# A hybrid decoder layer on one core: side work placed by a time model, the delta rule cut in two, 256-column weight blocks, scratch transfers on ScalarE's queue

## The chip, the core and the metric

The kernel runs on one core of a Trainium2 chip. The core has a matrix engine (TensorE, PE in the profile, with its weight loads as PEld), three engines for element-wise work (VectorE = DVE, ScalarE = ACT, GpSimd = POOL) and a synchronisation engine (SyncE = SP), which here issues DMA transfers. The metric is the device time of one execution in microseconds; lower is better. Before the change it is 1955.09 us, the median of three runs (1952.89 to 1960.22).

## What is computed

One inference step of one layer for two request groups that share all weights: a prompt of 256 tokens and 8 requests with one token each. Everything is float32.

```python
h = rmsnorm(x, norm_mix)
proj = h @ w_in                       # 2048 x 13344: pool, q, k, v, z, a, b, two gates
A = pool_mixer(proj[pool])            # trailing means over 2, 4, 8, 16 tokens, small products
q, k, v = silu(short_conv(proj[qkv])) # causal, width 4; q, k l2-normalised per head (16 heads of 128)
o, S = gated_delta_chunked(q, k, v, g, beta, S0)
#   per chunk: a_mat = strict_lower((k*beta) @ k.T * decay)
#              sol = solve(a_mat + I, [v*beta | k*beta*exp(gc)]); then products with S and q
gdn = rmsnorm(o) * silu(z)
x += (sig(gp)*(A @ w_pool_up) + sig(gg)*(gdn @ w_gdn_up)) @ w_o
x += (silu(f @ w_gate) * (f @ w_up)) @ w_down          # f = rmsnorm(x), inner width 5632
x += (p @ w_ple) * sig(x @ w_ple_gate);   y = rmsnorm(x)
```

It returns the 264 output rows and the new pooling, convolution and delta-rule states.

## The kernel before

**Weight products.** All 264 tokens are the moving columns of every matrix product. The weights come from memory in 592 blocks of 512 KB, two 128-row tiles by 512 columns each. `wload` (L244) issues a block on SP's queue into one of three buffers `wr`. `split` writes the rounded high part `wh` on ACT (L174) and the rest `wl` on DVE (L158), four buffers each. `gemm` then runs 24 products of 128x128x264 per block on PE (L183): each of 8 weight tiles gives high by high, high by low and low by high into an accumulator `acc`. There are about 14,160 of these products. Four accumulators of 512 columns are filled over all blocks of a column stripe, then evacuated.

**Side work.** All the rest (norms, convolution, delta rule, mixer, gates, state stores) is written as Python generators that hand back a step at a time. `tick`, called after each group of six products, moves these generators on by fixed counts of such slots (`yield -3` means three slots later, constants `W1` to `WD`) and by a budget of PE work. The scheduler then sets the order of each engine, except where program order is kept: PE's side products and transposes, SP's side DMAs, and everything on the side engines in the first of four head groups.

**The delta rule** (`gdn`) runs once for each of four groups of four heads, beside the weight products of the q, k, v and z stripes. Its chain of steps: the decay masks `dm`; transposes `kv` and products `pp` on PE; the matrix A (in `dm`). Then the diagonal 32x32 blocks of A are inverted on POOL: four DMAs of 32 KB put them in a scratch tensor `scr`; one DMA of 512 KB, named g<-scr, reads the 128 KB of `scr` four times over into 128 partitions; 31 dependent steps of a multiply and a subtract on POOL (L161, L158); a copy (L777); a DMA to a second scratch (scr<-g); four DMAs back (g<-scr, x4); a 32x32 transpose on DVE (L786). PE's products `px` and `py` then double the blocks to 128, and further products give outputs and states (`pu`, `po`, `pS`, `pk`, `pq`). All DMAs named here are on SP's queue. The last tokens of q, k and v leave by small tiles `tl`, filled by POOL (L626, L627), transposed on PE (`tlp`) and stored.

**After the delta rule** come the mixer, the sample tokens' delta rule (`kqp` and `pd` on PE, its states `S` loaded and stored in 512 KB pieces), the merges, out_proj, the feed-forward part and the embedding part.

Of the kernel before, what the change touches and what calls it, by code (L numbers as in the profile page):

```python
# [15 lines left out]
# slots between dependent steps of the work beside the weight products  # L16
W1, W2, W3 = 6, 3, 8
WA, WB, WC, WD = 5, 5, 6, 2
# [10 lines left out]
KB = 2  # L29
JS = 2  # L30
NL = 5
SIDE = ("DVE", "Activation", "Pool")
# [3 lines left out]
GH = 4  # L36


class Step:
    def __init__(self, ctx, tc, ins, outs):  # L40
# [8 lines left out]
        self.accp = ctx.enter_context(tc.tile_pool(name="accp", bufs=5, space=ps))  # L49
        self.psp = ctx.enter_context(tc.tile_pool(name="psp", bufs=3, space=ps))  # L50
        self.dp = ctx.enter_context(tc.tile_pool(name="dp", bufs=2, space=bass.MemoryType.DRAM))
        self.n = 0
        self.lanes = []
# [3 lines left out]
        self.wait = 0  # L57
        self.rate = 0.5
        self.budget = 0.0
        self.strm = self.stream()  # L60
        self.raws, self.pre = [], []
        self.LA, self.LD, self.LM = 1, 1, 3
        self.pins = SIDE
        self.nsp = 0
# [7 lines left out]
    # Keeps what was traced since n0 in program order on its engine.  # L72
    def pin(self, n0):
        ins = self.nc.cur_bb.bb.instructions
        for k in range(n0, len(ins)):
            e = ins[k].engine
            if str(e).split(".")[-1] in self.pins:
                for j in range(k - 1, -1, -1):
                    if ins[j].engine == e:
                        self.tc.add_manual_dep(ins[k], ins[j].name, mybir.DependencyInfo(  # L80
                            mybir.DependencyClass.NoSync, mybir.DependencyReason.DATA), reason="order")
                        break

    def step(self, gen):
        n0 = self.count()
        c = next(gen, None)
        self.pin(n0)
        if c is None:
            return True, 0
        if c > 0:  # L90
            self.budget -= c
            return False, 0
        return False, int(-c)

    def tick(self):
        self.budget = min(self.budget + self.rate, 2 * self.rate)
        for lane in list(self.lanes):
            lane[1] -= 1
            if lane[1] > 0:
                continue  # L100
            done, lane[1] = self.step(lane[0])
            if done:
                self.lanes.remove(lane)
        if self.post and self.budget > 0:
            cost, fn = self.post.pop(0)
            n0 = self.count()
            fn()
            self.pin(n0)
            self.budget -= cost
        if self.wait > 0:  # L110
            self.wait -= 1
        while self.main and self.budget > 0 and not self.wait:
            done, self.wait = self.step(self.main[0])
            if done:
                self.main.pop(0)

    def lane(self, gen):
        self.lanes.append([gen, 0])

    def drain(self):  # L120
        while self.post or self.lanes or self.main:
            self.budget = 1e9
            if self.post:
                self.post.pop(0)[1]()
# [5 lines left out]
        self.budget, self.wait = 0.0, 0  # L130
# [48 lines left out]
    def dma(self, out, in_):  # L179
        self.tc.keep_in_program_order(self.nc.sync.dma_start(out, in_))  # L180

    def mm(self, out, lhsT, rhs, start=True, stop=True, pin=True):
        ins = self.nc.tensor.matmul(out, lhsT, rhs, start=start, stop=stop)  # L183
        if pin:
            self.tc.keep_in_program_order(ins)

    def tr(self, out, in_):
        k = in_.shape[0]
        self.tc.keep_in_program_order(self.nc.tensor.transpose(out=out, in_=in_, identity=self.ident[:k, :k]))  # L189
# [10 lines left out]
    def stream(self):  # L200
# [3 lines left out]
        def cols(src, r0, K, c0, n=512):  # L204
            for k in range(0, K, KB):
                yield src, r0 + k, min(KB, K - k), c0, n
        wi = lambda c0: cols(w_in, 0, KT, c0)
        for hg in range(4):
            for part in (1, 0, 2, 3):
                yield from wi(1024 + part * D + hg * 512)  # L210
# [27 lines left out]
    def wload(self):  # L238
# [4 lines left out]
        raw = self.wp.tile([P, KB, 512], F32, tag="wr", name=self.nm("wr"), bufs=3)[:, :nk, :n]  # L243
        self.nc.sync.dma_start(raw, src[k0 * P:(k0 + nk) * P, c0:c0 + n].rearrange("(k p) c -> p k c", p=P))  # L244
        self.raws.append((raw, nk, n))

    def wsplit(self):
        n0 = self.count()
        raw, nk, n = self.raws.pop(0)
        hi = self.wp.tile([P, KB, 512], F32R, tag="wh", name=self.nm("wh"))[:, :nk, :n]  # L250
        lo = self.wp.tile([P, KB, 512], F32R, tag="wl", name=self.nm("wl"))[:, :nk, :n]
# [3 lines left out]
        if self.nsp == 1:  # L255
            self.pin(n0)
# [16 lines left out]
    def gemm(self, K, xh, xl, evac):  # L273
        accs = [self.accp.tile([P, 512], F32, tag="acc", name=self.nm("acc"))[:, :NT] for _ in range(4)]
        for k0 in range(0, K, KB):
            nk = min(KB, K - k0)
            wh, wl = self.wblock()
            for m in range(4):
                for kk in range(nk):
                    k = k0 + kk  # L280
                    h = wh[:, kk, m * P:(m + 1) * P]
                    l = wl[:, kk, m * P:(m + 1) * P]
                    self.mm(accs[m], h, xh[:, k], start=(k == 0), stop=False, pin=False)
                    self.mm(accs[m], h, xl[:, k], start=False, stop=False, pin=False)
                    self.mm(accs[m], l, xh[:, k], start=False, stop=(k == K - 1), pin=False)
                if k0 + nk == K:
                    evac(m, accs[m])
                self.tick()

    # ------------------------------------------------------------ constants  # L290
# [50 lines left out]
    def params2(self):  # L341
# [6 lines left out]
        yield -8  # L348
# [51 lines left out]
    # ------------------------------------------------------------ input norm  # L400
# [24 lines left out]
    def input_norm(self, x, xs):  # L425
# [50 lines left out]
        yield -4  # L476
# [9 lines left out]
    # ------------------------------------------------------------ decays  # L486
    def decays(self):
# [9 lines left out]
        yield -5  # L497
# [12 lines left out]
        ab = pool.tile([P, 3, 32], F32, name="ab", bufs=1)  # L510
# [15 lines left out]
        while self.post:  # L526
            yield -1
# [4 lines left out]
        yield -2  # L532
# [17 lines left out]
        yield -2  # L550
# [9 lines left out]
        g3 = pool.tile([P, 3, 32], F32, name="g3", bufs=1)  # L560
# [19 lines left out]
        self.dm = self.B("dm")[:, :H * TP].rearrange("p (h b c) -> p h b c", h=H, b=2)  # L580

        def mask(q):
            rm = self.e4("gm", F32R)[:96, :512].rearrange("p (j t) -> p j t", j=4)
# [919 lines left out]
```

## Time and profile before

| | |
|---|---|
| runs | 1952.89, 1955.09, 1960.22 us |
| span of the profiled execution, first to last instruction | 1954.1 us |
| PE busy | 1883.0 us, 96% of the span |
| weight loads | 1858.6 us, 95% |
| DVE, ACT, POOL busy | 1097.2 us (56%), 875.1 us (45%), 326.7 us (17%) |
| DMA | 344.93 MB, 177 GB/s on average |
| mean granted clock of PE | 0.982 of full speed |

The profiled execution's own time is its span, 1954.1 us, and what lies around it; the span is 1.0 us under the median of the runs. Busy times of different engines overlap and don't add up to the span. PE's clock has two levels here, 2.4 GHz (1.0) and 1.2 GHz (0.5), and a mean between them says for what share of a stretch each was granted.

### The profile page before, as it was taken

The numbers are of one execution on the slowest core, as the hardware profiler recorded it, in microseconds if no ns is written. First come the engines' busy times: TensorE is split into PE (matmuls) and PEld (weight loads), VectorE is DVE, ScalarE is ACT, GpSimd is POOL, SyncE is SP. The second block draws the span as 40 slices with busy tenths as digits, with TensorE's granted clock in tenths as the row PEclk, the third lists the DMA queues.
The fourth block names the chain that finished last, engine by engine and source line by source line (L and its number), as shares of the span: only waits on it lengthen the run. The fifth ranks groups of instructions, "written<-read, shape, count | busy, mean of one in ns | idle before, by whom it ended". The sixth has DMA issues, their size and how long they took to land.

```text
span 1954.1 us, 38176 instructions
## 1 busy us (share of the span) xinstructions
PE 1883.0 (96%) x15700; PEld 1858.6 (95%) x15700; DVE 1097.2 (56%) x1724; ACT 875.1 (45%) x1408; POOL 326.7 (17%) x628
## 2 busy tenths in 40 slices
PE   8998997989989999999999999999999999999997
PEld 7998997989989888999999999999999999999997
DVE  5764655646644876745565555544545544555554
ACT  6573543535534343444444444433444333444444
POOL 1325243251431322200011000000000000000011
PEclk9998998999989999999999999999999999999998
DMA  7555454544646678765655666556666556665553
GB/s 230 178 149 151 137 155 125 152 144 147 165 125 189 208 215 268 209 183 179 227 181 170 180 182 183 178 180 183 181 177 182 183 180 178 182 183 179 178 173 110
DMA packets 219058, 344.93 MB, mean 177 GB/s; under 512 B 26003, under 2 KB 65756, under 8 KB 218740
## 3 DMA queue, kind: packets, MB, share of 16 engines
q1 hardware_dynamic: 218883, 342.50, 58.8%
q8 instruction: 123, 2.02, 0.4%
q14 instruction: 52, 0.42, 0.1%
HBM read 327.28 MB, written 16.03 MB: 176 GB/s over the span
## 4 chain that ended last, share of the span: by engine, by line
PE 79%; DMA 7%; POOL 6%; issue 3%; DVE 2%; ACT 2%; SPq 0%; ACTq 0%; DVEq 0%; POOLq 0%
PE acc L183 74%; POOL g L158 3%; DMA g<-scr 3%; POOL g L161 2%; DMA out_dram<-S 2%; DMA wr<-in_w_in_dram 1%; DMA S<-in_state_ssm_dram 1%; PE pp L183 1%; PE px L183 1%; DVE wl L158 1%; ACT wh L174 1%; PE py L183 0%; SPq L180 0%; PE kv L189 0%; PE po L183 0%
## 5 line engine op out<-in xcount | busy, mean ns | idle before, releaser
L158 DVE TENSOR_TENSOR wl<-wr,wh 128x1024 fp32r<-128x1024 f32 x592 | 727.3, 1229 | 666.2 <-ACT wh L174 665.4
L174 ACT ACTIVATE wh<-wr 128x1024 fp32r<-128x1024 f32 x592 | 625.0, 1056 | 863.0 <-PE acc L183 666.1
L183 PE MATMUL acc<-hh,wh 128*128 128x264 f32 x1664 | 488.2, 294 | 0.4 <-ACT wh L174 0.4
L183 PE MATMUL acc<-hl,wh 128*128 128x264 f32 x1664 | 478.6, 288 | 0.0
L183 PE MATMUL acc<-hh,wl 128*128 128x264 f32 x1664 | 477.4, 288 | 0.0
L183 PE MATMUL acc<-xnh,wh 128*128 128x264 f32 x1408 | 400.4, 284 | 0.0
L183 PE MATMUL acc<-xnl,wh 128*128 128x264 f32 x1408 | 400.2, 284 | 0.0
L183 PE MATMUL acc<-xnh,wl 128*128 128x264 f32 x1408 | 400.1, 284 | 0.0
L183 PEld LDWEIGHTS acc<-hh,wh 128*128 128x128 f32 x1664 | 319.2, 192 | 4.0 <-issue 2.0
L183 PEld LDWEIGHTS acc<-hl,wh 128*128 128x128 f32 x1664 | 319.2, 192 | 1.2 <-issue 0.2
L183 PEld LDWEIGHTS acc<-hh,wl 128*128 128x128 f32 x1664 | 317.8, 191 | 0.6 <-issue 0.2
L183 PEld LDWEIGHTS acc<-xnh,wh 128*128 128x128 f32 x1408 | 265.4, 189 | 0.0
L183 PEld LDWEIGHTS acc<-xnl,wh 128*128 128x128 f32 x1408 | 265.0, 188 | 0.0
L183 PEld LDWEIGHTS acc<-xnh,wl 128*128 128x128 f32 x1408 | 264.5, 188 | 0.0
L183 PE MATMUL acc<-hidl,wh 128*128 128x264 f32 x704 | 200.1, 284 | 0.0
L183 PE MATMUL acc<-hidh,wl 128*128 128x264 f32 x704 | 200.1, 284 | 0.0
L183 PE MATMUL acc<-hidh,wh 128*128 128x264 f32 x704 | 200.1, 284 | 0.0
L161 POOL TENSOR_TENSOR gs<-gs,rb 128x264 f32<-128x264 f32 x44 | 45.6, 1047 | 630.7 <-ACT gs L171 630.7
L183 PEld LDWEIGHTS acc<-hidh,wh 128*128 128x128 f32 x704 | 132.7, 189 | 0.0
L183 PEld LDWEIGHTS acc<-hidl,wh 128*128 128x128 f32 x704 | 132.5, 188 | 0.0
L183 PEld LDWEIGHTS acc<-hidh,wl 128*128 128x128 f32 x704 | 132.2, 188 | 0.0
L155 POOL TENSOR_TENSOR ss<-ss,sst 128x264 f32<-128x264 f32 x28 | 25.3, 905 | 432.0 <-ACT sst L171 312.2
(364 smaller groups left out, 2605.2 us busy)
## 6 DMA issues: line engine op xcount, KB each, us to landing
wr<-in_w_in_dram SPq DMA_DIRECT2D x208, 512.0 KB
wr<-in_w_gate_up_dram SPq DMA_DIRECT2D x176, 512.0 KB
wr<-in_w_down_dram SPq DMA_DIRECT2D x88, 512.0 KB
wr<-in_w_gdn_up_dram SPq DMA_DIRECT2D x32, 512.0 KB
wr<-in_w_o_dram SPq DMA_DIRECT2D x32, 512.0 KB
wr<-in_w_ple_gate_dram SPq DMA_DIRECT2D x32, 512.0 KB
S<-in_state_ssm_dram SPq DMA_DIRECT2D x16, 512.0 KB
out_dram<-S SPq DMA_DIRECT2D x16, 512.0 KB
```

Of the source, the lines that this page charges most:

```text
L155: (eng or self.nc.vector).tensor_tensor(out=out, in0=a, in1=b, op=ALU.add)
L158: (eng or self.nc.vector).tensor_tensor(out=out, in0=a, in1=b, op=ALU.subtract)
L161: (eng or self.nc.vector).tensor_tensor(out=out, in0=a, in1=b, op=ALU.mult)
L174: self.nc.scalar.activation(out, a, AF.Copy)
L183: ins = self.nc.tensor.matmul(out, lhsT, rhs, start=start, stop=stop)
```

## The change

- **Placement.** A class `Model` keeps an estimated time for each engine and for each piece of memory written. A side step is traced as soon as the model's time of PE has passed the time at which its inputs are ready, and while DVE and ACT are estimated no more than `room` (6 us, later 4) behind PE. Every instruction of every engine is then pinned in the order in which it was traced.
- **Delta rule.** `gdn` becomes `gdn_a` (masks, k and q side, inversion) and `gdn_b` (everything that needs v or the inverse). They run as separate generators, `gdn_a` with two sets of buffers `gset` and the inversion in one further buffer `gone`. The masks are made for each head group instead of all at once.
- **Scratch transfers.** The four small DMAs to `scr`, the 512 KB read, the DMA to `scr2` and the four back are issued from ACT (`fast`).
- **Blocks.** A block is four 128-row tiles by 256 columns (512 KB still, 24 products still); two accumulators are filled at a time. Only the first stripe keeps 512 columns.
- **Engines.** The copies into `tl` and the copies of the sample tokens' q, k and v move from POOL to ACT, the addition of the convolution's old rows from POOL to DVE. ACT has 1419 instructions instead of 1305, DVE 1771 instead of 1721, POOL 454 instead of 626, SP 701 instead of 739; activation table loads are 17 instead of 13.

```diff
-KB = 2
+KB = 4
...
+class Model:
+    def cost(self, i, ins, out):
...
+            return 0.26 + 0.0022 * n, 0.10                    # Pool
...
+    def run(self, floor=0.0):
...
+            at = max([self.T[eng], floor] + [self.ready(b) for b in ins])
+            if type(i).__name__ == "InstDMACopy":
+                self.T[eng] = at + 0.06
+                n = max(self.free(b) * (b[2] - b[1]) for b in ins + out) * 4
+                end = max(self.ring.get(eng, 0.0), at) + n / 320e3
+                self.ring[eng] = end
+                end += 2.6
...
+    def at(self, ap):
+        self.note()
+        return (self.model.ready(self.model.boxed(ap)),)
+
     def tick(self):
...
+        for group in (self.lanes, self.post):
+            for lane in list(group):
+                n = 0
+                while lane[1] <= self.now and not self.behind() and n < 4:
+                    done, lane[1] = self.step(lane[0])
...
+    def fast(self, out, in_):
+        self.nc.scalar.dma_start(out, in_)
...
+            for c in range(c0, c0 + n, 256):
+                for k in range(0, K, KB):
+                    yield src, r0 + k, min(KB, K - k), c, 256
...
             def a():
-                nc.gpsimd.tensor_copy(tlv(0, 3)[:, m], u[:, 253:TP])
-                nc.gpsimd.tensor_copy(tlv(12, 8)[:, m], u[:, TP:NT])
                 self.scl(y, u, w(3))
+                self.copy(tlv[:, m], u[:, 253:NT])
...
-    def gdn(self, hg, q, k, v):
+    def gdn_a(self, hg, q, k):
...
-        while (2, hg) not in self.ready:
-            yield -1
-        for a, src in enumerate((k, q, v)):
-            nc.gpsimd.tensor_copy(self.qkv_s[:, a, h0:h0 + GH], src[:, :, TP:NT])
-        pt = four_t(v, 0)
-        yield -2
...
-            self.dma(scr[d].rearrange("a s c -> s a c"), A[r, :, r])
+            self.fast(scr[d].rearrange("a s c -> s a c"), A[r, :, r])
+        yield self.at(scr)
+        self.fast(at.rearrange("p s c -> p (s c)"),
+                  scr.rearrange("d a s c -> (d a) (s c)").unsqueeze(0).broadcast_to([4, 32, 1024]))
+        for j in range(31):
+            n, l = 31 - j, j // 4 + 1
+            tv = tm[:, :n * l].rearrange("p (a b) -> p a b", a=n)
+            self.mul(tv, at[:, j, j + 1:].unsqueeze(2).broadcast_to([P, n, l]),
+                     tw[:, j:j + 1, 0:l].broadcast_to([P, n, l]), nc.gpsimd)
+            self.sub(tw[:, j + 1:, 0:l], tw[:, j + 1:, 0:l], tv, nc.gpsimd)
+        nc.gpsimd.tensor_copy(twt, tw.rearrange("p i l -> p l i"))
+        yield self.at(twt)
+        scr2 = self.dp.tile([8, 4, 4, G8, 32], F32, tag="scr2", name=self.nm("scr2"))
+        self.fast(scr2.rearrange("l c d a i -> (c d a) l i"), twt)
+        yield self.at(scr2)
+        for d in range(4):
+            r = slice(32 * d, 32 * d + 32)
+            self.fast(Tt[r, :, r], scr2[:, :, d].rearrange("l c a i -> (l c) a i"))
...
+    def gdn_b(self, hg, q, k, v):
+        yield from self.await_((2, hg))
...
+        yield from self.await_(("inv", hg))
+        yield self.at(Tt)
         nc.vector.transpose(out=Tm.rearrange("p a c -> p (a c)"), in_=Tt.rearrange("p a c -> p (a c)"))
```

**Order on POOL and PE before.** The end of the inversion in the first head group stands so on POOL before the change (g2 is the buffer of the inversion, u a fresh k stripe, L777 the last copy):

```order
L161 TENSOR_TENSOR g2_191_1457<-g2_191_1457 128x8
L158 TENSOR_TENSOR g2_191_1457<-g2_191_1457 128x8
L626 COPY tl_235_1850<-u_264_2133 128x3
L627 COPY tl_235_1850<-u_264_2133 128x8
L777 COPY g2_191_1457<-g2_191_1457 128x256
L155 TENSOR_TENSOR k_233_1848<-k_233_1848,spre_338 128x8
L626 COPY tl_235_1850<-u_265_2145 128x3
L627 COPY tl_235_1850<-u_265_2145 128x8
```

The first two of the stripe's eight `tl` copies stand behind the inversion's 62 steps and ahead of its last copy, the others behind that. On PE before, the transpose of that `tl` and the first product on the inverse stand close together, `tlp` six weight products ahead of `px`:

```order
L189 MATMUL tlp_2318<-ident,tl_1850 44x128
L183 MATMUL acc_2172<-hh_155,wh_2213 128x264
L183 MATMUL acc_2172<-hl_156,wh_2213 128x264
L183 MATMUL acc_2172<-hh_155,wl_2214 128x264
L183 MATMUL acc_2172<-hh_155,wh_2213 128x264
L183 MATMUL acc_2172<-hl_156,wh_2213 128x264
L183 MATMUL acc_2172<-hh_155,wl_2214 128x264
L183 MATMUL px_2328<-g_190_1456,dm_993 32x32 x16
```

After the change neither copy stands on POOL, and `px` stands later: counted on PE, at 1320, 1848, 2424 and 3276 weight products from the start for the four head groups, 151, 174, 95 and 83 products behind the place at which the DMA to `scr2` is traced.

**Order on ACT after.** The two scratch transfers around POOL's work now stand between ACT's other instructions. The first head group's read of `scr` (gone is the inversion's buffer, wh the high parts of weight blocks, k the fresh k stripe of the next head group):

```order
L336 ACTIVATE wh_232_1813<-wr_220_1710 128x1024
L346 DMA scr_235_1831<-gset_82_617 32x8x32 x4
L336 ACTIVATE wh_236_1854<-wr_223_1740 128x1024
L339 ACTIVATE k_213_1701<-u_239_1872,cw_338 128x264
L336 ACTIVATE tl_215_1703<-u_239_1872 128x11
L339 ACTIVATE k_213_1701<-u_240_1888,cw_338 128x264
L336 ACTIVATE tl_215_1703<-u_240_1888 128x11
L336 ACTIVATE wh_243_1894<-wr_234_1817 128x1024
L346 DMA gone_84_619<-scr_235_1831 128x1x1024
L336 ACTIVATE wh_246_1996<-wr_238_1858 128x1024
```

And the write of the result, which waits for POOL's last copy, with what stands behind it:

```order
L336 ACTIVATE wh_297_2390<-wr_288_2322 128x1024
L346 DMA scr2_301_2430<-gone_84_619 128x8x32
L336 ACTIVATE tls_302_2432<-tlp_300_2418 44x128
L336 ACTIVATE wh_303_2434<-wr_291_2353 128x1024
L346 DMA gset_82_617<-scr2_301_2430 32x8x32 x4
L333 ACTIVATE q_212_1700<-q_212_1700 128x264 x2
L336 ACTIVATE wh_308_2478<-wr_299_2394 128x1024
```

On SP these five steps stood between block loads alone. On ACT, between the read of `scr` and the write of `scr2` stand 12, 10, 12 and 13 of the `wh` splits in the four head groups. The split just ahead of the read is first used by PE at its weight product 913, 1489, 2065 and 2929; the first split behind the write at 1225, 1753, 2377 and 3265. That is 312, 264, 312 and 336 products later. By the program's order the read is issued 4, 17, 7 and 1 products ahead of that first use. In the second head group about 8 us of the delta rule's own products stand on PE in that stretch too, in the third about 3.5 us, in the others next to nothing. Counted in weight products, a split stands on ACT 36 to 52 products ahead of its use on average in this stage (least 6), and on DVE 24 to 40 (least 2); before the change the averages were 72 and 65. In the feed-forward part they are about 59 and 50 after the change, and blocks are issued there about 108 products ahead of their use (125 before). At the end of the program four output transposes stand behind the last weight product instead of two.

## Rows read from the trace of the kernel before

**Rows 1.** Page, busy time of each engine, its share of the span, instructions.
```profile
PE 1883.0 (96%) x15700; PEld 1858.6 (95%) x15700; DVE 1097.2 (56%) x1724; ACT 875.1 (45%) x1408; POOL 326.7 (17%) x628
```

**Rows 2.** Windows by stage: length, busy PE, PEld, DVE, ACT, POOL, clock, DMA, GB/s.
```profile
0.00:612.00 612.00, 565.08 (x4782) 552.39 (x4783) 354.16 (x633) 312.74 (x677) 202.20 (x491) 0.96 0.54 155
612.00:806.00 194.00, 181.02 (x1593) 172.43 (x1592) 140.60 (x344) 69.23 (x94) 51.89 (x63) 0.99 0.77 228
806.00:1954.00 1148.00, 1136.93 (x9330) 1133.77 (x9328) 602.42 (x749) 493.13 (x637) 72.61 (x74) 1.00 0.59 179
```

**Rows 3.** Windows: a long stretch of the feed-forward part, a piece of the sample stage.
```profile
1100.00:1850.00 750.00, 750.00 (x6167) 750.00 (x6166) 381.03 (x449) 306.18 (x358) 41.68 (x40) 1.00 0.61 181
...
750.00:800.00 50.00, 47.71 (x419) 45.46 (x418) 36.47 (x90) 16.66 (x20) 15.43 (x12) 1.00 0.85 254
```

**Rows 4.** Waits of PE: what waited for what, us in total, times, longest.
```profile
PE px L183 <- DVE g L786: 25.1, 4, 8.7
PE tlp L189 <- POOL tl L627: 11.1, 3, 5.4
PE kqp L996 <- DMA S<-in_state_ssm_dram: 10.3, 8, 3.5
...
PE dmp L183 <- ACT dm L171: 1.8, 1, 1.8
...
PE dmp L183 <- POOL gm L161: 1.0, 1, 1.0
```

**Rows 5.** Windows of 20 us around the end of each inversion; one ahead.
```profile
175.00:195.00 20.00, 12.19 (x140) 11.43 (x139) 8.87 (x12) 6.75 (x11) 5.76 (x25) 0.74 0.60 166
299.00:319.00 20.00, 9.08 (x74) 8.48 (x72) 8.28 (x11) 5.72 (x9) 6.94 (x31) 0.66 0.51 148
425.00:445.00 20.00, 11.17 (x126) 10.35 (x125) 8.36 (x11) 5.73 (x9) 5.50 (x25) 0.66 0.59 171
551.00:571.00 20.00, 11.34 (x137) 10.88 (x136) 7.29 (x8) 5.61 (x6) 3.47 (x14) 0.74 0.63 171
...
500.00:550.00 50.00, 50.00 (x416) 49.99 (x415) 24.94 (x43) 21.47 (x35) 25.50 (x50) 1.00 0.52 141
```

**Rows 6.** Chain of waits into the first px: start us, us, what.
```profile
179.28 2.24 DMA scr<-g
...
182.89 1.90 DMA g<-scr
...
184.91 1.26 DVE g L786
```

**Rows 7.** Longest pieces of the whole chain: the four reads of scr, a block load.
```profile
137.18 10.82 DMA g<-scr
...
260.82 13.15 DMA g<-scr
...
387.92 10.20 DMA g<-scr
429.59 3.88 DMA wr<-in_w_in_dram
...
512.80 11.81 DMA g<-scr
```

**Rows 8.** Timeline of POOL, fourth inversion: first and last of its 63 instructions.
```profile
524.68 0.24 POOL L161 TENSOR_TENSOR g<-g 128x31 f32<-128x31 f32 x1 [20.14 <-DMA g<-scr]
...
554.84 0.63 POOL L777 COPY g<-g 128x256 f32<-128x256 f32 x1
```

**Rows 9.** Timeline of SP, same place: issue of the four transfers back.
```profile
557.75 1.81 SPq L180 DMA_DIRECT2D g<-scr  x4
```

**Rows 10.** Groups by line: instruction xcount, total us, mean ns, idle before it.
```profile
L158 DVE TENSOR_TENSOR wl<-wr,wh 128x1024 fp32r<-128x1024 f32 x592 | 727.3, 1229 | 666.2 <-ACT wh L174 665.4
L174 ACT ACTIVATE wh<-wr 128x1024 fp32r<-128x1024 f32 x592 | 625.0, 1056 | 863.0 <-PE acc L183 666.1 <-DMA wr<-in_w_in_dram 108.0 <-issue 40.6
L171 ACT ACT_TABLE_LOAD x12 | 15.4, 1283 | 5.2 <-DVE k L164 5.1
```

More of the change, by code (lines that the diff above doesn't have):

```diff
@@ L74, in pin @@
         ins = self.nc.cur_bb.bb.instructions
[L75 to L82, printed above, removed]
+        for k in range(self.npin, len(ins)):
+            i = ins[k]
+            e = str(i.engine)
+            if type(i).__name__.startswith("Bass"):
+                continue
+            j = self.lastof.get(e)
+            if j is not None:
+                self.tc.add_manual_dep(i, j, mybir.DependencyInfo(
+                    mybir.DependencyClass.NoSync, mybir.DependencyReason.DATA), reason="order")
+            self.lastof[e] = i.name
@@ L84, in step, with note, now, behind @@
+        self.npin = len(ins)
+    def note(self, floor=0.0):
+        t = self.model.run(floor)
+        self.pin()
+        return t
+    @property
+    def now(self):
+        return self.model.T["PE"]
+    def behind(self):
+        T = self.model.T
+        return max(T["DVE"], T["Activation"]) - T["PE"] > self.room
     def step(self, gen):
-        n0 = self.count()
+        self.note()
         c = next(gen, None)
-        self.pin(n0)
+        t = self.note()
         if c is None:
-            return True, 0
@@ L90, in step @@
[L90 to L93, printed above, removed]
-    def tick(self):
[L96 to L112, printed above, removed]
+            return True, 0.0
@@ new lines, in step @@
+        if c == "stored":
+            return False, self.model.stored + 0.5
+        if isinstance(c, tuple):
+            return False, c[0]
+        if c < -1:
+            self.skip[id(gen)] = -c
+            return False, 0.0
+        return False, (0.0 if c > 0 else t)
+    def at(self, ap):
+        self.note()
+        return (self.model.ready(self.model.boxed(ap)),)
+    def tick(self):
+        self.note()
+        for gen in list(self.paced):
+            n = self.skip.get(id(gen), 1) - 1
+            self.skip[id(gen)] = n
+            if n <= 0 and self.step(gen)[0]:
+                self.paced.remove(gen)
+        n = 0
+        while self.main and self.wait <= self.now and not self.behind() and n < 4:
@@ L209, in stream @@
             for part in (1, 0, 2, 3):
-                yield from wi(1024 + part * D + hg * 512)
+                if part == 1 and hg == 0:
+                    yield from wide(w_in, KT, 1024 + D)
+                else:
+                    yield from wi(1024 + part * D + hg * 512)
         yield from wi(9248)
@@ L254, in wsplit @@
         self.pre.append((hi, lo))
-        if self.nsp == 1:
-            self.pin(n0)
+        self.splits.append(self.note(self.now))
         self.LA = min(self.LA + (self.nsp > NL), self.LM)
@@ L679, in gdn @@
+        if hg > 1:
+            yield from self.await_(("gdn", hg - 2))
+        st = self.sets[hg % 2]
+        qk, dm, Tt, Kt, tm = (st[n] for n in ("qk", "A", "Tt", "Kt", "tm"))
         col = lambda b: slice(b * P, (b + 1) * P)
         small = lambda n, sh: gw.tile(sh, F32, tag=n, name=self.nm(n), bufs=2)
-        so = small("so", [P, 2, 2, GH])
-        junk = gw.tile([P, P], F32, tag="junk", name=self.nm("junk"), bufs=1)
-        def four_t(src, g):
-            pt = self.ps("kv").rearrange("p (h b c) -> p h b c", h=2, b=2)
-            for hh in range(2):
-                for b in range(2):
-                    self.tr(pt[:, hh, b], src[:, 2 * g + hh, col(b)])
-            return pt
+        rms = []
@@ L692, in gdn @@
+        yield -1
+        for b in range(2):
+            for j in range(4):
+                self.act(dm[:, j, b], pms[b][:, j], AF.Exp, bias=self.ngc[:, b * H + h0 + j:b * H + h0 + j + 1])
+        yield 0.5
+        so = small("so", [P, 2, 2, GH])
         for a, src in enumerate((k, q)):
-            while (1 - a, hg) not in self.ready:
+            yield from self.await_((1 - a, hg))
+            for g in range(2):
+                pt = self.four_t(src, g)
                 yield -1
-            for g in range(2):
-                pt = four_t(src, g)
-                yield -2
```

523 lines of the change are left out of this document (328 added, 195 removed).

## Prediction

> **What bounds the kernel now.** I read the page first: PE and its weight loads are busy 96% and 95% of the span, and no other engine is above 56% [rows 1]. So PE sets the time, and a gain must come from PE's idle time, from a lower clock, or from fewer cycles. The windows by stage tell where the idle time is: 612 - 565.1 = 46.9 us while the delta rule runs, 13.0 us in the sample stage, 11.1 us in the remaining 1148 us [rows 2]. In the feed-forward stretch PE has no idle time at full clock, 750 us for 6167 products, 0.1216 us each [rows 3]. That work is the same after the change, 24 products a block, so nothing is to be had there.
>
> The waits of PE name what the idle time of the first stage is: 25.1 us in four waits of `px` for DVE's transpose (L786), the end of the inversion, and 11.1 us in three waits of `tlp` for POOL's `tl` copies; the sample stage has 10.3 us of `kqp` for a load of states [rows 4]. The windows around the four ends of the inversion show PE idle 7.8, 10.9, 8.8 and 8.7 us of 20, together 36.2 = 25.1 + 11.1, and a mean clock of 0.74, 0.66, 0.66 and 0.74, where the 50 us ahead of one have PE full at 1.00 [rows 5]. The clock has two levels, so the lower one was granted for 20 x 2 x (0.26 + 0.34 + 0.34 + 0.26) = 48 us. It follows the wait: PE idles, the clock falls, and work goes on at half speed for some microseconds. If nearly all of px's 25.1 us lie at the lower level, 23 us of work ran there, and half of that, 11.5 us, was lost.
>
> **What the change removes.** The transpose before `px` comes late because the inversion is long and `px` is placed by slots, only six products behind `tlp` on PE. After the change `px` is traced when the model thinks the inverse is there, 83 to 174 products (10 to 21 us) behind the place of the DMA to `scr2`. Its own tail is a DMA of 2.24 us, four of 1.90 us and a transpose of 1.26 us [rows 6], plus 1.81 us of issue for the four [rows 9]: 7.2 us. So px's wait goes, unless PE waits elsewhere (below): -25.1. The `tl` copies leave POOL, where they stood behind the 62 steps: -11.1. The clock's loss goes with them: -11.5. Sum -47.7 us.
>
> **What the scratch DMAs on ACT cost.** A DMA issued on ACT waits in ACT's order. The DMA to `scr2` waits for POOL's last copy, and the `wh` splits behind it wait too, hence `wl` and PE. On SP only loads stood behind it. How long may it wait? From the read of `scr` to PE's first use of a block split behind the write, PE has 312, 264, 312 and 336 products, 37.9, 32.1, 37.9 and 40.9 us at 0.1216. With about 8 us of side products in the second group and 3.5 us in the third, and the 0.5, 2.1, 0.9 and 0.1 us of weight products by which the read is ahead of the first use, that makes 38.4, 42.2, 42.3 and 41.0 us.
>
> What must fit in there: the 512 KB read took 10.82, 13.15, 10.20 and 11.81 us [rows 7]. The fourth substitution runs from 524.68 to 555.47, 30.8 us [rows 8], the pace of POOL at present. Then one split on ACT, 1.06 us, and one on DVE, 1.23 us [rows 10], of which two products (0.24 us) hide some: 2.05 us. The read's price on a queue of its own no row shows; its bounds are 3.88 us, the block load of the same size [rows 7], and 13.15 us. I take 10.2 us, the shortest row of the same transfer, since it is the same four-fold read and only the blocks queued ahead of it go. Need: 10.2 + 30.8 + 2.05 = 43.05 us. PE waits 4.7, 0.9, 0.8 and 2.1 us, together 8.4.
>
> The Trainium skill bears on this choice ("DMA: Bandwidth & Descriptors", section "Issuing engines are not separate DMA queues"): DMAs started from different engines share the same 16 DMA engines, and starting them elsewhere saves only the time to issue. Its "Rules for kernel authors" add that a leading zero-stride dimension of c copies, as this read has with c = 4, confines the transfer to at most c engines. By both the read stays near the 10 to 13 us that the rows show and the sum is the one below; if the queue made the difference, it would be the 1907 us of the first rival. The trace before agrees in this: a block load of the same bytes took 3.88 us, the read 10.2 to 13.15.
>
> Behind that write the next four DMAs wait for it in turn. The second split behind it comes 2.24 us + 1.81 us + one table load or a few small activations (about 1 us, from the 1.283 us row [rows 10]) + 1.06 + 0.99 = 7.1 us after it, while PE needs it 2.05 + 24 x 0.1216 = 5.0 us after it. That is 2.1 us for each of three groups; in the fourth `px` comes 11 products behind, at 3.4 us, where its tail needs 7.2: 3.8 us. Together 10.1, so the ACT queue costs 8.4 + 10.1 = 18.5 us of PE idle. Before, 36.2 us of idle cost 11.5 us of clock, a ratio of 0.32; here 5.9. Sum +24.4 us.
>
> **The other edits.** The model's placement lets masks, which waited 1.8 and 1.0 us [rows 4], come ahead of need: -2.8. In the sample stage each of three changes of head group still stores a state and loads another into the same buffer before `kqp`, about 3 us each (the longest now is 3.5 [rows 4]): of 13.0 us idle 10 stay: -3. Splits are placed 36 to 52 products ahead on ACT instead of 72, and ACT gets more to do in the first stage: about 60 small copies of 0.35 us, 36 DMA issues of 0.45 us, five table loads of 1.283 us [rows 10], 44 us on 312.7 busy of 612 [rows 2]. It is not full, but where six products (0.73 us) are the lead and both splits take 2.3 us, PE waits 1.6 us; two or three such places: +4. At the end four output transposes instead of two remain behind the last product: +1. The 256-column blocks halve the length of a row's run in memory at the same bytes. I cost that at nothing: blocks need 181 GB/s at a share of 0.61, and the sample stage, with states in runs of 512 bytes among them, moved 254 GB/s at 0.85 [rows 3], and blocks are issued 108 products (13 us) ahead. If that cover were gone, a share beyond 1 would stretch all of the feed-forward part; doubling 0.61 would give 1.22, so this is a mishap to look for. Pinning every order and the change of accumulators to two of four buffers cost nothing that a row shows.
>
> **Sum.** -47.7 + 24.4 - 2.8 - 3 + 4 + 1 = -24.1. From the profiled span, 1954.1, that is 1930.0; the median of the runs is 1.0 above the span: **1931 us**. A measurement of this kernel can tell about 0.5%, 9.8 us, from no change.
>
> **Rivals.**
> *Full gain.* The read on its own queue takes a block's time, 3.88 us. Then 3.9 + 30.8 + 2.05 = 36.8 us are needed, less than any of the four distances, and ACT never stops PE: the 24.4 us fall away, 1907 us. For it: every read of before stood on SP among block loads. Against it: the four-fold read is another transfer than a block, and all four rows lie between 10 and 13 us. Without the +4 and +1, and with the sample stage's other 10 us gone, it would be 1892.
> *No gain.* The ACT queue takes the place of `px`. With a read of 13.15 us, 46.0 us are needed; PE waits 7.6 + 3.8 + 3.7 + 5.0 + 10.1 = 30.2 us, with clock 39.9, and with late splits at twice my price 1950 us. For it: the model reckons the read at 512 KB / 320 GB/s + 2.6 = 4.2 us, and so places the write 6 to 9 us too early on ACT. Against it: POOL has less to do, so its 30.8 us may shrink.
> *Slower.* Splits late all through the first stage. DVE's splits are 24 to 40 products (2.9 to 4.9 us) ahead on average, and a pair takes 2.3 us, so every bunch of small work of more than 0.6 to 2.6 us reaches PE. The four head groups have 4 x 4 x 8 = 128 blocks; at 0.35 us each this costs 45 us in place of my 4: 1972 us. It decides from 0.34 us a block, where the time passes 1965. Against it: DVE was busy 58% and ACT 51% of that stage [rows 2], and the order leaves no engine beyond two thirds.
>
> **How the numbers follow.** Chances: this sum 0.45 (1912 to 1945), full gain 0.25 (1890 to 1912), no gain 0.15, slower 0.15. The range must leave out no more than 2 in 10: it drops the slower case and the far end of the full gain, 1890 to 1962. Faster by over 0.5% (below 1945.3) are the first two, 0.70; within 0.5% is the no gain, 0.15; slower 0.15.
>
> **What would show it.** In the profile after: no wait of `tlp` for `tl`; waits of `px` gone but for the fourth head group; instead three or four waits of `acc` for `wh` or `wl` of 1 to 6 us, just after POOL's last copy, with ACT's DMA queue as what held the split, and the clock at its lower level there for some 20 us rather than 48. The read of `scr` at 9 to 12 us would bear out the sum; at 4 us, the first rival. A first stage of about 590 us instead of 612 goes with 1931. Waits of `acc` on `wl` spread over all blocks would make me wrong to the slow side; a feed-forward stretch above 0.1216 us a product would mean the narrower blocks cost something that I put at nothing.

## The result

The changed kernel took 1973.75 us (median, 1970.33 to 1974.73), the kernel before 1957.26 in the same comparison: a ratio of 1.0081, interval 1.0054 to 1.0108. It is slower by about 16 us where 1931 us, 26 us less, was forecast. The profiled execution has a span of 1968.6 us.

PE has 10 us more busy time for the same 15,700 products, and the span is 14.5 us longer (page, busy time by engine):

```profile
PE 1893.4 (96%) x15700; PEld 1860.1 (94%) x15700; DVE 1113.2 (57%) x1774; ACT 883.3 (45%) x1482; POOL 256.6 (13%) x456
```

The windows by stage (columns as in [rows 2]) show in which stages it is lost: the first 50 us, the delta rule's stage with them, the sample stage, the rest, and the feed-forward stretch:

```profile
0.00:50.00 50.00, 36.35 (x189) 29.84 (x189) 18.89 (x42) 25.47 (x54) 3.61 (x28) 0.90 0.47 142
0.00:625.00 625.00, 573.18 (x4740) 554.44 (x4741) 368.05 (x680) 323.31 (x740) 154.36 (x334) 0.96 0.53 149
625.00:820.00 195.00, 186.19 (x1642) 176.82 (x1641) 145.10 (x327) 71.86 (x101) 44.47 (x47) 1.00 0.80 230
820.00:1968.00 1148.00, 1134.01 (x9324) 1128.85 (x9322) 600.07 (x768) 488.16 (x641) 57.76 (x75) 0.99 0.58 180
1100.00:1850.00 750.00, 750.00 (x6195) 750.00 (x6194) 382.84 (x452) 305.19 (x360) 30.31 (x40) 1.00 0.58 181
```

In the first 50 us of the kernel before, the same view has:

```profile
0.00:50.00 50.00, 42.51 (x304) 37.80 (x305) 29.22 (x58) 29.86 (x64) 6.12 (x36) 1.00 0.72 230
```

So 115 products fewer are done in the first 50 us, at a lower clock: a loss at a place of which the prediction did not speak. The first 625 us have 51.8 us of idle time where the first 612 had 46.9 [rows 2]; behind the first 50 us that is 38.2 against 39.4, so of the delta rule's waits next to nothing is gone. The clock of that stage is 0.96 as before, so its share did not come back either. The sample stage went about as forecast (8.8 us idle instead of 13.0), the rest has 14.0 us idle instead of 11.1, and the feed-forward stretch did not suffer: 6195 products in 750 us against 6167 [rows 3].

The waits of PE from 110 to 612 us have new names (us in total, times, longest):

```profile
PE ot L353 <- DVE gone L330: 10.6, 4, 6.2
PE tlp L353 <- ACT tl L336: 4.9, 2, 4.1
PE kv L353 <- ACT gset L333: 4.7, 2, 3.3
PE acc L349 <- ACT wh L336: 3.0, 1, 3.0
PE pp L349 <- DVE go L326: 2.8, 1, 2.8
PE px L349 <- DVE gone L993: 2.6, 1, 2.6
PE dmp L349 <- POOL gm L323: 2.3, 2, 2.1
```

`px` waits 2.6 us instead of 25.1 and `tlp` 4.9 instead of 11.1 [rows 4]. But `ot`, the transposes that end a head group's output, wait 10.6, and seven kinds of step share some 31 us where two had 36.2. POOL's timeline at the second inversion, its first and last instruction and what follows, tells why `ot` waits:

```profile
277.76 0.24 POOL L323 TENSOR_TENSOR gset<-gone 128x31 f32<-128x31 f32 x1 [17.69 <-DMA gone<-scr]
...
308.06 0.63 POOL L947 COPY gone<-gone 128x256 f32<-128x256 f32 x1
308.65 1.65 POOL L362 TENSOR_TENSOR osc<-so,mhalf 128x8 f32<-128x8 f32 x1
310.26 1.04 POOL L323 TENSOR_TENSOR gm<-gcT,dmask 96x512 fp32r<-96x512 f32 x1
```

`osc`, the factor of the output norm of the head group before, and `gm`, a mask product of the next one, stand right behind the last copy of the inversion. This inversion takes 30.9 us on POOL, the other three 34.4, 33.1 and 32.8, where the prediction had 30.8 from one row [rows 8]. At the third inversion it is the same (copy at 416.44, `osc` at 417.03), and there `ot` has its longest wait, 6.2 us. PE's transpose follows 1 us of DVE later (PE's timeline):

```profile
311.44 0.69 PE L353 MATMUL ot<-ident,gone 128*128 128x128 f32 x2 [3.82 <-DVE gone L330]
```

The chain of waits gives the four reads of `scr` on ACT's queue:

```profile
168.45 11.44 DMA gone<-scr
...
265.87 11.75 DMA gone<-scr
...
371.56 12.27 DMA gone<-scr
...
514.31 12.43 DMA gone<-scr
```

They are as long as on SP (10.20 to 13.15 [rows 7]). The model in the kernel reckons 4.2. The Trainium skill says in "DMA: Bandwidth & Descriptors", section "Issuing engines are not separate DMA queues", that transfers issued from different engines run on the same 16 DMA engines; the trace agrees with it in that ACT's queue made the read no shorter.

And ACT waits for the inversion, as predicted, at the first and the fourth write to `scr2`; at the second and third it waits longer, and for `osc` (ACT's timeline):

```profile
214.42 0.39 ACTq L346 DMA_DIRECT2D scr<-gone  x1
214.86 0.27 ACT L336 ACTIVATE tls<-tlp 44x128 f32<-44x128 f32 x1 [5.35 <-POOL gone L947]
...
310.34 0.40 ACT L339 ACTIVATE gone<-gone,osc 128x128 f32<-128x128 f32 x1 [11.10 <-POOL osc L362]
...
418.71 0.40 ACT L339 ACTIVATE gone<-gone,osc 128x128 f32<-128x128 f32 x1 [8.20 <-POOL osc L362]
...
560.22 1.06 ACT L336 ACTIVATE wh<-wr 128x1024 fp32r<-128x1024 f32 x1 [4.32 <-POOL gone L947]
```

A block is late beside the read, too. While the first read is under way, a split on ACT waits 6.23 us for its block (with the read as four transfers, below, 2.23 at most there); the `tl` copies stand behind that split, and `tlp` has 4.1 of its 4.9 us there:

```profile
180.81 1.06 ACT L336 ACTIVATE wh<-wr 128x1024 fp32r<-128x1024 f32 x1 [6.23 <-DMA wr<-in_w_in_dram]
```

### The profile page after: what moved, and what is told of

Same layout as the page of the kernel before. It is cut to its first block, busy times and chain, and to the rows that moved or that the text cites. A ratio compares the mean times of both kernels' runs of the same rounds, so it can differ in the third digit from the quotient of the medians.

```text
span 1968.6 us, 38101 instructions
## 1 busy us (share of the span) xinstructions
PE 1893.4 (96%) x15700; PEld 1860.1 (94%) x15700; DVE 1113.2 (57%) x1774; ACT 883.3 (45%) x1482; POOL 256.6 (13%) x456
## 4 chain that ended last, share of the span: by engine, by line
PE 73%; DVE 7%; DMA 7%; POOL 6%; ACT 4%; issue 3%; ACTq 1%; SPq 0%; POOLq 0%; DVEq 0%
PE acc L349 68%; POOL gset L323 3%; POOL gone L320 3%; DMA gone<-scr 2%; DVE wl L320 2%; ACT wh L336 2%; DMA S<-in_state_ssm_dram 1%; DVE gset L326 1%; DMA wr<-in_w_pool_up_dram 1%; DVE S L326 1%; ACTq L346 1%; DMA xd<-xT 0%; ACT gset L333 0%; PE xt L353 0%; PE kv L353 0%
## 5 line engine op out<-in xcount | busy, mean ns | idle before, releaser
L320 DVE TENSOR_TENSOR wl<-wr,wh 128x1024 fp32r<-128x1024 f32 x594 | 713.7, 1222 | 544.2 <-ACT wh L336 541.8
L336 ACT ACTIVATE wh<-wr 128x1024 fp32r<-128x1024 f32 x594 | 609.0, 1047 | 454.2 <-PE acc L349 118.5
L323 POOL TENSOR_TENSOR gs<-gs,rb 128x264 f32<-128x264 f32 x44 | 33.3, 758 | 640.4 <-ACT gs L333 640.4
L317 POOL TENSOR_TENSOR ss<-ss,sst 128x264 f32<-128x264 f32 x28 | 21.2, 758 | 425.5 <-ACT sst L333 299.8
```

The costliest lines, as they stand in the source:

```text
L317: (eng or self.nc.vector).tensor_tensor(out=out, in0=a, in1=b, op=ALU.add)
L320: (eng or self.nc.vector).tensor_tensor(out=out, in0=a, in1=b, op=ALU.subtract)
L323: (eng or self.nc.vector).tensor_tensor(out=out, in0=a, in1=b, op=ALU.mult)
L336: self.nc.scalar.activation(out, a, AF.Copy)
```

## The experiments

Theory A had two parts: the pinned order costs at the start, and the model places everything behind the inversion too early, since it prices the read at 4.2 us and, as was added later, POOL's 62 steps and copy at 62 x 0.26 + 3120 columns x 0.0022 + 0.8 = 24 us instead of 31 to 34. The rivals were late loads, ACT's queue, the shape of the blocks, and the form of the read.

**The first stripe left to the scheduler.**

```diff
+        if self.free:                 # weight products of the first stripe,
+            self.npin = len(ins)      # and splits 2 to 8: not pinned
+            return
```

> Edit: in the changed kernel, the weight products of the first stripe and the seven splits behind the first are left to the scheduler instead of being pinned; all else is pinned as it was. Theory A (the loss at the start is the pinned order: ACT does the second block's split only behind the norm work, at 17.70 us instead of 10.98 us before, and PE is 16.5 us behind at its 150th weight product): most of the 16.5 us come back, 1958 to 1964 us, and the 150th weight product starts at 41 to 45 us instead of 57.7. Rival B (the start is slow because blocks or tokens arrive late, 142 GB/s in the first 50 us against 230 before): the order doesn't matter, within 4 us of 1974.

1961.52 us, 1.0004 (0.999 to 1.0018) of before: about 15 us less than the changed kernel. The first 50 us are those of before again:

```profile
0.00:50.00 50.00, 43.34 (x302) 38.60 (x302) 27.72 (x55) 31.56 (x70) 3.61 (x28) 1.00 0.70 228
```

With loads and tokens as they were, DMA moves 228 GB/s instead of 142 once the order is free: the loads were late because they were asked for late. Rival B falls.

**Only the splits of the first stripe earlier**, every pin kept.

```diff
                     self.tick()
+                    if wide is not None and m == 1 and not self.pre:
+                        if not self.raws:
+                            self.wload()
+                        self.wsplit()
```

> Edit: the changed kernel, still pinned throughout, but each split of the first stripe is traced after the second of the four column groups of the block ahead of it instead of behind the fourth. If the loss at the start is that splits stand too late on ACT and DVE (PE waits about 2.3 us for each, wh 4.4 and wl 3.9 us named, at the lower clock in between): 1959 to 1965 us, as with the first stripe left to the scheduler. If it is the pinned order of PE's products and transposes: above 1969 us.

1965.57 us, 1.0029 (1.0017 to 1.004), at the edge of what was expected: about 10 of the 15 us. In the changed kernel the second split stands behind the norm's work of six tiles on ACT and starts at 17.70 us, where it started at 10.98 before (ACT's timeline of each):

```profile
17.32 0.48 ACT L339 ACTIVATE hh<-xt,nmcol 128x264 fp32r<-128x264 f32 x1 [0.34 <-PE xt L353]
17.70 1.05 ACT L336 ACTIVATE wh<-wr 128x1024 fp32r<-128x1024 f32 x1
```

```profile
10.98 1.06 ACT L174 ACTIVATE wh<-wr 128x1024 fp32r<-128x1024 f32 x1 [2.41 <-DMA wr<-in_w_in_dram]
```

What PE waits for in the first 60 us of the changed kernel says the same:

```profile
PE acc L349 <- ACT wh L336: 4.4, 3, 2.0
PE acc L349 <- DVE wl L320: 3.9, 5, 1.1
```

So two thirds are the splits' place; the rest is other pinned order there, not taken apart.

**The read priced as it is**, and a second edit with it: `gst`, what the second part of the delta rule waits for before it transposes v, is set before the inversion instead of after it.

```diff
-                end = max(self.ring.get(eng, 0.0), at) + n / 320e3
+                slow = out and out[0][0].startswith("gone")
+                end = max(self.ring.get(eng, 0.0), at) + n / (55e3 if slow else 320e3)
```

> Edit: the model's price of the four-fold read of scr is 512 KB / 55 GB/s + 2.6 = 12.1 us instead of 4.2, as the trace has it (11.4 to 12.4 us), and v's transposes no longer wait for the inversion to be traced. Theory A (the model places what follows the inversion some 8 us too early, and PE waits in it: ot 10.6, tlp 4.9, kv 4.7, acc on wh 3.0, px 2.8, dmp 3.3 us in the first stage, with clock about 38 us): most of that goes, 1940 to 1955 us. Rival C (ACT and DVE are late all through the stage because the pinned order leaves splits short leads): the waits only change their names, 1966 to 1976 us.

1955.68 us, 0.9963 (0.9947 to 0.9978), some 23 us less than the changed kernel by the ratios, though the start is still slow. `ot` waits 3.4 us instead of 10.6. Rival C is not borne out. How the 23 us divide between the price and `gst` this run does not show.

**The read as four transfers.**

```diff
-        self.fast(at.rearrange("p s c -> p (s c)"),
-                  scr.rearrange("d a s c -> (d a) (s c)").unsqueeze(0).broadcast_to([4, 32, 1024]))
+        for c in range(4):
+            self.fast(at[32 * c:32 * c + 32].rearrange("p s c -> p (s c)"),
+                      scr.rearrange("d a s c -> (d a) (s c)"))
```

> Edit: in the changed kernel, the 512 KB read of scr (one transfer that names the 128 KB four times) becomes four transfers of 128 KB on the same queue, each to a quarter of the partitions; nothing else. Theory E (the read is slow by its form, and its length is what the model gets wrong): the four land within 4 to 6 us instead of 11.4 to 12.4, the model's 4.2 us is about right, the waits of ot, kv and dmp behind the inversion shrink, 1945 to 1960 us. Rival F (the read is slow because it shares the transfer engines with the block loads, whatever its form): it stays at 10 us or more, and the time within 5 us of 1974.

1960.68 us, 1.0006 (0.9989 to 1.0023), 15 us less, just beyond the slow end of what theory E expected. The pieces of the read in the chain of waits are 3.7 to 6.4 us, but each is the last of four transfers; from the first one's issue to POOL's first step it is 5.1 to 7.9 us, where the single read has 11.6 to 12.6:

```profile
170.44 5.86 DMA gone<-scr
...
263.26 3.68 DMA gone<-scr
...
507.49 6.41 DMA gone<-scr
```

The same bytes by the same queue beside the same loads: the form of the read made it slow, and rival F falls.

**The same in the kernel before.**

> Edit: the kernel before with the read of scr as four transfers on SP's queue; nothing else. Theory E with the prediction's reading of before (36.2 us of waits at the four ends of the inversion, 11.5 us of clock with them): each inversion ends some 7 us earlier, so 28 of the 36 us go, with clock 37: 1918 to 1930 us. Theory E with px placed by slots after other late steps: part only, 1930 to 1945. Rival F: the read stays at 10 us or more, 1953 to 1961 us.

1937.94 us, 0.988 (0.9851 to 0.9909). One edit, and 23 us. PE's waits:

```profile
PE px L183 <- DVE g L787: 21.1, 4, 6.5
...
PE tlp L189 <- POOL tl L627: 1.6, 2, 1.3
```

`tlp` and `px` together fall from 36.2 to 22.7 us; with the clock's share of the prediction that is 13.5 x 1.32 = 18 us. The two profiled executions differ by as much, 1954.1 and 1936.3 us of span; the 23 us of the medians are more because the profiled execution of before is one of its faster ones.

**The `tl` copies on ACT in the kernel before**, one copy for two.

> Edit: the kernel before with the copies into tl on ACT instead of POOL (one copy for two), alone. The prediction's step (11.1 us of waits of tlp go away with the copies, and part of the clock's loss): 1940 to 1947 us. Theory A2 (px stands six products behind tlp and waits for the same inversion, so the wait of tlp is only the first part of one wait): px waits 36 us instead of 25, and the time stays within 4 us of 1957.

1963.23 us, 1.0017 (1.0001 to 1.0033): no gain. Its waits of PE, in a profiled execution 7 us above that median:

```profile
PE px L183 <- DVE g L785: 26.8, 4, 7.9
PE tlp L189 <- ACT tl L174: 17.1, 3, 6.6
```

The wait of `tlp` does not leave with POOL, since ACT in its turn waits for POOL there, with the later copies behind it (ACT's timeline at the first inversion):

```profile
185.69 0.42 ACT L171 ACTIVATE k<-k 128x264 f32<-128x264 f32 x1 [14.07 <-POOL k L155]
```

A2 has the time right, and not the place, since `px` keeps its wait and `tlp` waits longer. The copies alone are worth nothing. What this run leaves on POOL is the addition that ACT waits for, which the change moves to DVE; copies and addition together were not tried.

**The blocks alone in the kernel before.** `KB = 4`, 256 columns, two accumulators, the first stripe as it was.

> Edit: the kernel before with 256-column blocks of four row tiles alone (first stripe still 512 columns); placement, queues and engines as before. Theory A (the block's shape costs nothing, the feed-forward part runs 0.1217 us a product either way): 1952 to 1962 us. Rival D (rows of half the length make block loads late while scratch and states move): 1965 us or more, with more waits of ACT's splits for block loads.

1967.77 us, 1.0034 (1.0021 to 1.0048), slightly slower, as rival D has it, but not in the place that it names. The feed-forward stretch is the changed kernel's:

```profile
1100.00:1850.00 750.00, 750.00 (x6195) 750.00 (x6194) 387.94 (x450) 305.06 (x358) 45.47 (x41) 1.00 0.59 182
```

The loss is in the delta rule, where `acc` waits for `wh` 30.2 us in five waits and `px` only 10.1. Three of the five are 6.5, 12.0 and 10.5 us, and ahead of each ACT waits, with splits behind, for POOL's addition to k, which stands behind the inversion: 11.74, 17.78 and 17.67 us (ACT's timeline at the second):

```profile
320.58 0.84 ACT L171 ACTIVATE k<-k 128x264 f32<-128x264 f32 x2 [17.78 <-POOL k L155]
```

So it is the order on ACT, and not late loads. That the narrow shape led the scheduler to this order is likely, but not shown. The changed kernel has this addition on DVE, and its ACT has no such wait; with 512-column blocks it was not tried.

**The scratch transfers on SP in the changed kernel** (`fast` issues on SP).

> Edit: in the changed kernel, the scratch transfers go back to SP's queue at the place in the order at which ACT issued them; nothing else. Theory A (the steps behind the inversion are traced too early for the read's real length; whichever queue holds the write to scr2 stops what is behind it): now block loads stop behind it, and the time stays or rises, 1968 to 1985 us. Rival C (ACT's queue itself is the cost, since splits stand behind the write): the waits of kv and dmp for ACT go, 1955 to 1965 us.

1983.41 us, 1.0113 (1.008 to 1.0145), 6 us slower than on ACT; `px` waits 14.1 us instead of 2.8. Rival C falls: as things are placed, ACT is the better queue.

**Start and read together.**

> Edit: the changed kernel with the first stripe left to the scheduler (as in the first experiment), the read of scr as four transfers, and v's transposes not waiting for the inversion to be traced. Theory A and E: the two losses are apart in time and add, 13 us at the start and 15 to 28 in the delta rule: 1932 to 1947 us. Rival: what is won at the start is lost again at the first inversion, 1950 to 1960 us.

1934.39 us, 0.9864 (0.9834 to 0.9893). That is more than the sum: by the ratios the free start alone is worth 0.0077 and the four reads alone 0.0075, and both together 0.0217, so some 13 us are left over. The third part of this edit is `gst` before the inversion, as in the run with the read priced. The last step of the delta rule on POOL, `osc` of the fourth head group, in the changed kernel, with the free start, with the four reads, and here (POOL's timeline of each):

```profile
607.58 1.64 POOL L362 TENSOR_TENSOR osc<-so,mhalf 128x8 f32<-128x8 f32 x1 [47.89 <-DVE so L326]
```

```profile
592.07 1.64 POOL L366 TENSOR_TENSOR osc<-so,mhalf 128x8 f32<-128x8 f32 x1 [47.70 <-DVE so L330]
```

```profile
593.80 1.64 POOL L362 TENSOR_TENSOR osc<-so,mhalf 128x8 f32<-128x8 f32 x1 [47.67 <-DVE so L326]
```

```profile
570.71 1.64 POOL L366 TENSOR_TENSOR osc<-so,mhalf 128x8 f32<-128x8 f32 x1 [46.61 <-DVE so L330]
```

It comes 15.5 and 13.8 us earlier by either edit and 36.9 by the whole, so 7.6 of the 13 us are gained before it. `ot`, which waits 10.2 us with the free start and 7.9 with the four reads, waits 3.4 here. So a third loss is likely: v's transposes stood behind the inversion for no need. No run has that edit alone.

**The same with the scratch transfers on SP.**

> Edit: as the run with the free start and four reads (1934 us), but with the scratch transfers on SP's queue. With steps placed nearly right, theory A gives little to either queue: 1932 to 1944 us. The prediction's price of ACT's queue (18.5 us of PE idle, 24 with clock) would make SP better by 10 us or more: below 1925. If block loads behind the write to scr2 are the worse thing to stop: 1944 or more.

1941.91 us, 0.991 (0.9887 to 0.9933), 7.5 us slower than on ACT by the medians, 9 by the ratios. So ACT's queue has no price of 24 us against SP's.

**Start and the read's price, the slow read kept.**

> Edit: the changed kernel with the first stripe left to the scheduler, the read of scr priced at 12.1 us in the model, and v's transposes not waiting; the read itself as it was. If the loss in the delta rule came from the wrong price, a right price does most of what a shorter read does: 1938 to 1946 us. If the length of the read itself matters too (block loads and splits late while it runs: tlp behind a split that waits 6.2 us for its block), it stays above the run with four reads by more than 5 us, 1940 to 1948; if only the price matters, 1932 to 1937.

1938.37 us, 0.9884 (0.9863 to 0.9905): 4 us above the four reads, both with `gst` set early. Against the run with the read priced and the slow start, the free start is worth 0.0079 here and 0.0077 alone: the start and the delta rule's losses add. With the price right, what a shorter read brings beyond it, 4 us, is not clear of the noise.

**POOL's price, with start and four reads.**

```diff
-            return 0.26 + 0.0022 * n, 0.10
+            return 0.36 + 0.0022 * n, 0.10
```

> Edit: as the run with the free start and four reads, and the model's price of a POOL instruction raised from 0.26 to 0.36 us + 0.0022 a column (the 62 steps and the copy then cost about 31 us, as the trace has them, instead of 25). Theory A (what is left of waits behind the inversion, ot 3.4, dmp 3.8, px 3.3, pp 3.9 us, is placed too early by the price of POOL): 1922 to 1930 us. Rival: these waits come from other engines' bunches, 1931 to 1938.

1924.57 us, 0.982 (0.9797 to 0.9842), 9 us less than without by the ratios and the fastest version here: 35 us below the kernel before. In its first stage 595 us hold 4907 products with 21.5 us idle:

```profile
0.00:595.00 595.00, 573.48 (x4907) 559.72 (x4908) 375.38 (x697) 328.14 (x748) 169.49 (x337) 0.99 0.58 165
```

From 110 to 612 us its largest waits are `pp` 2.5, `acc` 2.3 and `dmp` 2.0; `ot` and `px` are no longer among them.

**Both prices, the slow read kept.**

> Edit: the changed kernel with the first stripe left to the scheduler, the slow read kept as it was, the read priced at 12.1 us and POOL at 0.36 us + 0.0022 a column, v's transposes not waiting. If the two prices were all that the model had wrong: within 4 us of the run with four reads and the POOL price (1925 us). If the read's 12 us themselves delay block loads and splits: 1930 to 1938 us.

1927.09 us, 0.9832 (0.9816 to 0.9849), within 2.5 us of four reads. What the read's length itself still costs once it is priced is not clear of the noise. The largest wait is `tlp`, whose 4.3 us at the first read are again behind a split that waits for its block, here 7.41 us (in a profiled execution 7 us above the median):

```profile
PE tlp L358 <- ACT tl L341: 4.7, 2, 4.3
PE pu L354 <- DVE gone L331: 3.5, 2, 3.3
```

**px ten slots later in the kernel before with four reads.** `WC` 16 instead of 6.

> Edit: the kernel before with four reads of scr (1938 us) and the slots ahead of px raised from 6 to 16 (WC), 60 to 150 weight products later; nothing else. If px's remaining 21.1 us in four waits are only a matter of where it stands, they go with their clock: 1910 to 1922 us. If the later steps of the delta rule then pile up at the end of the stage, where no weight products hide them: 1925 to 1940.

1940.82 us, 0.9896 (0.9874 to 0.9917), no better than without. All of px's 21.1 us are gone from the waits of PE, and these stand there instead:

```profile
PE acc L183 <- DVE wl L158: 7.3, 6, 2.3
PE tlp L189 <- POOL tl L627: 5.7, 2, 4.2
PE acc L183 <- ACT wh L174: 4.0, 2, 3.7
```

They add up to 17. Counted slots moved one step rightly and put others in each other's way.

## Why the prediction was wrong, step by step

**The pinned orders.** The sentence "pinning every order ... cost nothing that a row shows" is the step that failed first. It reached for no row of the first 50 us. In that stretch the scheduler had set the second split at 10.98 us; the pinned order set it behind the norm's work. Measured: 15 us back by leaving the first stripe free, 10 by moving the splits alone. A term put at nothing makes up 15 of the 42 us between forecast and result.

**-47.7 us for the waits.** The wait of `px` did go (25.1 to 2.6), by the reason given. That the time goes with it was the error: the steps behind it took the wait over, `ot` above all, since the model has the inversion end 15 to 18 us before it does (7 to 8 for the read, 7 to 11 for POOL). The prediction had read the 4.2 us of the model in its second rival, but let it act only on ACT's order. POOL's own order, where `osc` and `gm` stand behind the 62 steps, and PE's placement of all that follows, were left out. The shorter read gives 15 us back, and POOL's price 9 us beside it; the read's price gave 23 us together with the earlier `gst`, whose share is open. The 11.5 us for the clock did not come either, since PE idles as much as before in that stage. With both prices right, `gst` early and the start free the kernel takes 1927 us, next to the 1931 forecast; that is no support for the sum, whose terms came out otherwise.

**-11.1 us for `tlp`.** Not borne out as a separate term: the copies alone are worth nothing, and in the changed kernel `tlp` still waits 4.9 us, 4.1 of them behind a split whose block is late beside the read.

**The read at 10.2 us, POOL at 30.8.** The read is right against the first rival, and 1 to 2 us too low; 11.4 to 12.4 was measured. POOL did not get faster with less to do: 30.9 to 34.4 us.

**+18.5 us for ACT's queue.** The wait is there, 5.35 and 4.32 us of ACT at the first and fourth write, and the longest wait of `kv`, 3.3 us, comes some microseconds behind the first; but ACT's longer waits, 11.10 and 8.20 us, are for `osc`, which the prediction did not have, and `acc` waits for late splits only 4.4 us from 110 to 612 us. Against SP the queue is 6 to 9 us to the good, so it is not what ate the gain, and that SP is the cheaper holder of a waiting transfer was wrong.

**Masks, blocks, sample stage, end.** -2.8 us for the masks did not come: `dmp` waits 3.3 us. No cost of the blocks in the feed-forward part: right, 750 us hold no fewer products. -3 us in the sample stage: -4.2. +1 at the end: `yt` waits 3.7 us instead of 1.0.

**The rivals.** *Full gain* fell with the read's length. *No gain* had the cause and half its reach. *Slower* had nearly the time, 1972, but by luck, since its mechanism is not there: waits of `acc` for `wh` and `wl` are 16.2 us in all, 8.3 of them in the first 60 us, not spread over the blocks.

## What to carry to other kernels

When a change pins orders that a scheduler had set, read the stretches in which that scheduler had put work ahead of its trace order, the start first. A planner is as good as its prices: compare each price with the duration in the trace before crediting the planner with a gain, and follow a wrong one on every queue that holds work behind it, not on one. A wait that leaves one step is gained only if the step behind it isn't waiting for the same thing.

## What was not expected of the hardware

One transfer that reads 128 KB four times over took 10.2 to 13.2 us, in the kernel before on SP's queue and in the changed one on ACT's; four transfers of 128 KB, for the same bytes, took 5.1 to 7.9 us from the first issue to POOL's first step, on either queue. The Trainium skill has the form in "DMA: Bandwidth & Descriptors", "Rules for kernel authors": a leading zero-stride dimension of c copies confines the transfer to at most c engines. These runs show the times, not which engines carried them.
